# A negated copy and its accumulating DMA ahead of the high part, and a way-down product one slot sooner, in a float32 encoder trunk on one core

## The chip, the cores and the metric

The kernel runs on one core of one Trainium2 chip. The metric is the device time of one execution in microseconds (us); smaller is better. A time below is either the median of several runs or that of the one execution that the profiler recorded.

## The reference

Two layers on 512 tokens of width 1024, all in float32. Each layer is: a half-step SwiGLU feed-forward network (FFN), a mixer (an mLSTM in layer 0, a gated MLP in layer 1), a second half-step FFN, and a gated per-layer input (PLE). After each of them comes a layer norm of the scaled residual.

```python
def swiglu_ffn(x, w_gu, w_d):
    g, u = jnp.split(x @ w_gu, 2, axis=-1)
    return (jax.nn.silu(g) * u) @ w_d
...
x = layer_norm(DN_ALPHA * x + 0.5 * swiglu_ffn(x, ffn1_wgu[i], ffn1_wd[i]), ln_g[i, 0], ln_b[i, 0])
x = layer_norm(DN_ALPHA * x + mix, ln_g[i, 1], ln_b[i, 1])
x = layer_norm(DN_ALPHA * x + 0.5 * swiglu_ffn(x, ffn2_wgu[i], ffn2_wd[i]), ln_g[i, 2], ln_b[i, 2])
ple = jax.nn.sigmoid(x @ ple_wg[i] + ple_bg[i]) * (p[i] @ ple_wp[i])
x = layer_norm(DN_ALPHA * x + ple, ln_g[i, 3], ln_b[i, 3])
```

The hidden width of an FFN is 2816, that is 22 blocks of 128. There are four FFNs: the first and third come before a mixer and are called *plain* here, the second and fourth come before a PLE.

## The kernel before

**Two-part products.** A float32 product is made of three fp32r products (`mm3`, L386): high by high, high by low and low by high. Each weight tile is split for this: the high part `whi` is a rounding copy on ScalarE (ACT, L275), the low part `wlo` is the weight less its high part. The low part is made in one of two ways. Either VectorE (DVE) subtracts (L284, or L290 where it is put off), or "by DMA": ACT writes a negated copy of the weight into `wlo` (L281), and GpSimd (POOL) issues a DMA that adds the weight to it (L282); the tile's type rounds the copy, so what is left is the low part.

**The order of the weights.** The class `Weights` (L50) holds one list for the whole program, `W.order`. `fill` (L247) goes through it strictly in order: it takes the next entry if a split tile of its kind is free ("main": 4 tiles, "rows": 2, "rowsx": 1 and others) and if its load has been issued, and it stops at the first entry that can't be had. So whenever a product has given its tile back with `W.release`, the splits of later weights are queued on ACT, far ahead of their use, behind whatever ACT was given before. Loads go through SyncE's (SP's) queue; a load's place among three raw tiles comes free when the splits of what stood there are done (`load`, L184). While `W.apart` is set, which it is in the chunks named next, a low part that DVE makes is put off: `W.lows` (L303) does it at the next slot, in order. In this state `fill` also stops at a load that was issued in the last two slots (L257).

**The FFN.** The hidden blocks go in six chunks of 2, 4, 4, 4, 4, 4 blocks. From the third chunk on (index 2, `UP_FROM`), `up_products` (L1128) makes the way up of four blocks in 14 slots, s = 0 to 13. They are two pairs of blocks with seven products each, r = s mod 7, a Strassen-like scheme of seven products in place of eight. I call the up product of slot s U0 to U13. Woven between them are the seven products of the way down of the chunk before, by the same scheme; I call them G1 to G7. Before the change, G comes after the up product of every odd slot, so G7 comes after U13.

In a slot the program gives out, in this order: the up product on TensorE (PE); `group.add` (L973), which adds the G of an earlier slot to the residual `xt` on DVE (L763); for r = 6 the gating of the first half of the tokens (`gated(1)`, which needs nothing of U13: DVE L1104, then a split, ACT and DVE, L393 and L394); `pair.take(r)`, which takes the product out (for r = 6 this is `gated(0)`, the second half by the same steps); `W.lows`; `W.release`, which fills; the SiLU where r is 1 or 5 (L1099); and where a G belongs to the slot, `group.product`, `W.release(kind="rows")`, which fills again, and the next form.

**Which low parts are by DMA.** `up_forms` (L129) marks them by r: 1, 3, 4, 5, 6 in a chunk's first pair, 1, 3, 5, 6 in its second. Elsewhere (mLSTM and gated MLP) `release(low="dma")` does so.

**The end of the FFN.** In the last chunk the way down of its own four blocks is made by `down` (L789), right after slot 13. It goes over four blocks of tokens, t = 0 to 3, with four weights each, d0 to d3, two matmul triples for each. `hs` is what `gated` has split: d2 and d3 are multiplied by what slots 7 to 13 made. The weights d0 to d3 come from two loads (two weights each), and their kinds are main, rows, rowsx, rows in a plain FFN and rowsx, rows, main, main ahead of a PLE. In W.order they stand after the weight of G7, and ahead of a PLE a pair of transposes of p (`turn_p`, tile `ptp`) stands between. After d3 come the weights of the next stage: the input projection of the mLSTM or the gated MLP in a plain FFN, `ple_wp` ahead of a PLE.

## Time and profile before

| | |
|---|---|
| median of 3 runs | 2194.01 us (2192.73 to 2197.59) |
| the profiled execution | 2193.39 us |
| its span, first to last instruction | 2191.7 us |
| TensorE (PE) busy | 2170.3 us, 99% of the span |
| VectorE (DVE) busy | 1760.5 us, 80% |
| ScalarE (ACT) busy | 1208.1 us, 55% |
| GpSimd (POOL) busy | 226.3 us, 10% |
| granted TensorE clock | 0.999 |

A profile page gives the busy time of each engine, the chain of work that ended last, and groups of instructions by source line. A matmul row names its tiles: `ups` is an up product of the last four chunks, `gps` a way-down product of the scheme, `dps` a product of `down`, and `wlo`, `whi` the two parts of a weight. In a timeline row the numbers are the start within the span and the duration, both in us, and in brackets the idle time of the engine before it and what ended that. Rows of one kind that follow each other are merged, with their count behind the x; a q behind an engine's name means that the row is an issue of a DMA.

### The profile page before, as it was taken

Reading aid. Unit: us, or ns where it says so; the run is one execution under the profiler, and the core shown is the slowest. Engines: PE = TensorE matmul, PEld = TensorE weight load, DVE = VectorE, ACT = ScalarE, POOL = GpSimd, SP = SyncE. Lnnn points to the kernel's source line nnn. Section 1 sums busy time; section 2 is a strip of 40 time slices with the busy share of each in tenths; the row PEclk is TensorE's granted clock in tenths of the full one; section 3 lists DMA queues with packets and bytes.
Section 4 is the critical chain, followed back from the end, with each engine's and each line's share of the span. In section 5 each row is a group of like instructions: output and inputs, shape, how many; then the busy total and the mean of one; then the engine's idle time right before and its main releaser. Section 6 shows DMA issues by size and latency. Waiting matters only on the chain.

```text
span 2191.7 us, 32537 instructions
## 1 busy us (share of the span) xinstructions
PE 2170.3 (99%) x12821; PEld 1922.0 (88%) x12821; DVE 1760.5 (80%) x2532; ACT 1208.1 (55%) x1668; POOL 226.3 (10%) x279
## 2 busy tenths in 40 slices
PE   9999999999999999999999999999999999999998
PEld 8899997888888889999888899997888888999987
DVE  5898877786767789888887998877788679988887
ACT  4576656454546445667444566655345553666642
POOL 1011100011101101111000011110001100111100
PEclk9999999999999999999999999999999999999999
DMA  6587764366857426887531587754437743777651
GB/s 187 156 204 184 172 153 136 92 154 128 155 130 154 135 81 163 200 194 172 173 125 58 153 207 186 176 145 135 144 77 140 168 135 116 179 191 179 135 183 58
DMA packets 228097, 329.46 MB, mean 150 GB/s; under 512 B 9140, under 2 KB 163892, under 8 KB 227944
## 3 DMA queue, kind: packets, MB, share of 16 engines
q1 hardware_dynamic: 169104, 211.83, 29.8%
q0 software_dynamic: 52224, 100.86, 27.5%
q10 hardware_dynamic: 6616, 14.69, 1.9%
q8 instruction: 101, 1.65, 0.3%
q14 instruction: 52, 0.43, 0.1%
HBM read 224.58 MB, written 2.11 MB: 103 GB/s over the span
## 4 chain that ended last, share of the span: by engine, by line
PE 78%; DVE 11%; issue 4%; ACT 4%; DMA 3%; SPq 0%; POOL 0%; DVEq 0%; ACTq 0%; POOLq 0%
PE ups L390 7%; PE ups L388 7%; PE ups L389 7%; PE gps L388 6%; PE gps L389 6%; PE gps L390 6%; DMA wlo<-wbox 2%; PE dps L389 2%; PE dps L390 2%; PE dps L388 2%; DVE wlo L290 2%; PE fps L388 2%; PE fps L389 1%; PE fps L390 1%; ACT whi L275 1%
## 5 line engine op out<-in xcount | busy, mean ns | idle before, releaser
L275 ACT ACTIVATE whi<-wbox 128x1024 fp32r<-128x1024 f32 x224 | 235.7, 1054 | 242.2 <-DVE wbox L141 96.9
L390 PE MATMUL ups<-xh,wlo 128*128 128x256 f32 x1024 | 290.3, 284 | 3.2 <-DMA wlo<-wbox 3.2
L388 PE MATMUL ups<-xh,whi 128*128 128x256 f32 x1024 | 289.9, 283 | 0.0
L389 PE MATMUL ups<-xl,whi 128*128 128x256 f32 x1024 | 289.7, 283 | 0.0
L275 ACT ACTIVATE whi<-wraw 128x1024 fp32r<-128x1024 f32 (+1 forms) x212 | 217.3, 1046 | 96.7 <-DVE wraw L119 22.6
L388 PE MATMUL gps<-whi,fhi 128*128 128x512 f32 x644 | 253.0, 393 | 0.4
L389 PE MATMUL gps<-wlo,fhi 128*128 128x512 f32 x644 | 252.2, 392 | 0.0
L390 PE MATMUL gps<-whi,flo 128*128 128x512 f32 x644 | 251.4, 390 | 0.0
L282 POOL DMA_DIRECT2D wlo<-wbox x144 | 122.2, 848 | 1076.8 <-ACT wlo L281 705.0
L763 DVE TENSOR_TENSOR xt<-xt,gps 128x512 f32<-128x512 f32 x302 | 194.9, 680 | 26.7 <-PE gps L390 26.7
L284 DVE TENSOR_TENSOR wlo<-wraw,whi 128x1024 fp32r<-128x1024 f32 (+1 forms) x140 | 167.6, 1214 | 41.8 <-ACT whi L275 40.9
L390 PEld LDWEIGHTS ups<-xh,wlo 128*128 128x128 f32 x1024 | 196.2, 192 | 4.3 <-DMA wlo<-wbox 4.2
L388 PEld LDWEIGHTS ups<-xh,whi 128*128 128x128 f32 x1024 | 196.1, 192 | 3.8 <-ACT us L1085 1.6
L389 PEld LDWEIGHTS ups<-xl,whi 128*128 128x128 f32 x1024 | 196.1, 192 | 2.3
L275 ACT ACTIVATE whi<-wquarter 128x1024 fp32r<-128x1024 f32 (+1 forms) x140 | 135.3, 966 | 77.0 <-DVE wquarter L119 28.9
L281 ACT ACTIVATE wlo<-wbox 128x1024 fp32r<-128x1024 f32 x144 | 150.4, 1044 | 0.0
L390 PEld LDWEIGHTS gps<-whi,flo 128*128 128x128 f32 x644 | 120.9, 188 | 26.9
L388 PEld LDWEIGHTS gps<-whi,fhi 128*128 128x128 f32 x644 | 121.3, 188 | 23.9 <-issue 1.6
L389 PEld LDWEIGHTS gps<-wlo,fhi 128*128 128x128 f32 x644 | 121.3, 188 | 21.6
L944 DVE TENSOR_TENSOR flo<-h,fhi 128x512 fp32r<-128x512 f32 (+1 forms) x140 | 88.5, 635 | 57.6 <-ACT fhi L941 57.0
L290 DVE TENSOR_TENSOR wlo<-wquarter,whi 128x1024 fp32r<-128x1024 f32 x104 | 126.6, 1218 | 0.0
L388 PE MATMUL fps<-xh,whi 128*128 128x512 f32 x288 | 112.2, 390 | 0.0
(365 smaller groups left out, 5822.4 us busy)
## 6 DMA issues: line engine op xcount, KB each, us to landing
wlo<-wbox POOLq DMA_DIRECT2D x144, 512.0 KB, 5.8
wbox<-in_ffn_wgu_dram SPq DMA_DIRECT2D x128, 512.0 KB, 4.9
wquarter<-in_ffn_wd_dram SPq DMA_DIRECT2D x64, 512.0 KB, 5.8
wraw<-in_ml_w_in_dram SPq DMA_DIRECT2D x24, 1024.0 KB, 5.8
wlo<-wraw POOLq DMA_DIRECT2D x48, 512.0 KB, 6.4
wraw<-in_ffn_wgu_dram SPq DMA_DIRECT2D x15, 1024.0 KB, 6.0
wraw<-in_gm_w_in_dram SPq DMA_DIRECT2D x15, 1024.0 KB, 5.6
wraw<-in_ffn_wgu_dram SPq DMA_DIRECT2D x17, 512.0 KB, 4.8
```

Of the source, the lines that this page charges most:

```text
L275: self.nc.scalar.activation(hi[:, s], src[:, s], AF.Copy)
L281: self.nc.scalar.activation(lo[:, s], src[:, s], AF.Copy, scale=-1.0)
L282: self.nc.gpsimd.dma_start(lo[:, s], src[:, s], accum_op=OP.add)
L284: self.nc.vector.tensor_sub(lo[:, s], src[:, s], hi[:, s].bitcast(F32))
L290: self.nc.vector.tensor_sub(lo, src, hi.bitcast(F32))
L388: mm(ps, st[0], mv[0], start=start, stop=False, skip_group_check=more)
L389: mm(ps, st[0], mv[1], start=False, stop=False, skip_group_check=more)
L390: mm(ps, st[1], mv[0], start=False, stop=stop, skip_group_check=more)
L763: vec.tensor_add(dst, dst, ps)
L944: vec.tensor_sub(lo, src, hi.bitcast(F32))
```

## The change

Three edits. First, in `fill`, a low part by DMA has its negated copy and its DMA issued before the high part's copy; before, the high copy came first. Second, in the second pair of the last chunk, the low part of r = 5 (U12) is no longer by DMA; DVE subtracts it, at the next `W.lows`. Third, in the last chunk G7 comes after U12, not after U13, and its weight stands before that of U13 in W.order.

```diff
@@ -45,6 +45,7 @@
 UP_BY_DMA = (1, 3, 4, 5, 6)
 UP_BY_DMA_2 = (1, 3, 5, 6)
+UP_BY_DMA_LAST = (1, 3, 6)
@@ -272,15 +273,16 @@
             for i in range(parts):
                 s = slice(i * shape[1] // parts, (i + 1) * shape[1] // parts)
+                by_dma = make in self.by_dma or low == "dma" and make not in self.in_place
+                if by_dma:
+
+                    self.nc.scalar.activation(lo[:, s], src[:, s], AF.Copy, scale=-1.0)
+                    self.nc.gpsimd.dma_start(lo[:, s], src[:, s], accum_op=OP.add)
                 self.nc.scalar.activation(hi[:, s], src[:, s], AF.Copy)
                 if meanwhile and make in self.in_place:
                     meanwhile()
                     meanwhile = None
-                if make in self.by_dma or low == "dma" and make not in self.in_place:
-
-                    self.nc.scalar.activation(lo[:, s], src[:, s], AF.Copy, scale=-1.0)
-                    self.nc.gpsimd.dma_start(lo[:, s], src[:, s], accum_op=OP.add)
-                elif not self.apart:
+                if not by_dma and not self.apart:
                     self.nc.vector.tensor_sub(lo[:, s], src[:, s], hi[:, s].bitcast(F32))
@@ -471,6 +473,10 @@
+    def down_after(c, s):
+
+        return s == 12 if c == LAST and s > 11 else s % 2 == 1
@@ -499,10 +505,10 @@
-                                            by_dma=UP_BY_DMA if b == starts[c] else UP_BY_DMA_2)
+                                            by_dma=UP_BY_DMA if b == starts[c] else UP_BY_DMA_2 if c < LAST else UP_BY_DMA_LAST)
                 for s, product in enumerate(products):
                     W.order.append(product)
-                    if s % 2:
+                    if down_after(c, s):
                         W.order.append(down_w.popleft())
@@ -1147,7 +1153,7 @@
                     W.release()
                     pair.gate(r)
                     W.form_ahead(3)
-                    if s % 2:
+                    if down_after(c, s):
                         group.product()
                         W.release(kind="rows")
                         group.form(True)
```

## The prediction

> **What bounds the kernel now.** I read the page first, then what TensorE (PE) waits for, then the timelines of the four FFN ends, engine by engine.

> ```profile
> span 2191.7 us, 32537 instructions
> PE 2170.3 (99%) x12821; PEld 1922.0 (88%) x12821; DVE 1760.5 (80%) x2532; ACT 1208.1 (55%) x1668; POOL 226.3 (10%) x279
> PE dps L389 <- DVE wlo L290: 4.8, 4, 1.6
> PE ups L390 <- DMA wlo<-wbox: 3.9, 6, 1.0
> PE ups L390 <- DMA wlo<-wbox: 0.3, 1, 0.3
> PE ups L390 <- DMA wlo<-wbox: 0.5, 1, 0.5
> PE ups L390 <- DMA wlo<-wbox: 0.4, 1, 0.4
> ```

> PE is busy or pipelined nearly all the time, and none of its work goes away: the change can only take or add waits of PE. Two kinds bear on it (third and fourth line: total us, times, longest). `down` waits once in each FFN for a low part made by DVE, and six up products wait for an accumulating DMA. The last three lines are windows of the third chunk (first, second and fourth FFN); the other three of the six lie in the last chunks, at U12.

> A matmul's row is longer than its pitch, so each such idle time hides a little more delay. The rows:

> ```profile
> 1052.48 0.28 PE L388 MATMUL ups<-xh,whi 128*128 128x256 f32 x1
> 1055.36 0.28 PE L388 MATMUL ups<-t_whi,whi 128*128 128x256 f32 x1
> 1077.35 0.40 PE L388 MATMUL gps<-whi,fhi 128*128 128x512 f32 x1
> 1079.87 0.39 PE L390 MATMUL gps<-whi,flo 128*128 128x512 f32 x1
> 1080.10 0.39 PE L388 MATMUL dps<-whi,wquarter 128*128 128x512 f32 x1
> 1081.47 0.50 PE L388 MATMUL dps<-whi,wquarter 128*128 128x512 f32 x1
> 1082.86 0.50 PE L389 MATMUL dps<-wlo,wquarter 128*128 128x512 f32 x1 [0.89 <-DVE wlo L290]
> ```

> The first two span an up product: 24 matmuls in 2.88 us, 0.12 each against 0.28 shown, so an idle time stands for 0.16 more. The next two and the first `dps` row are G7 of the second FFN: 2.75 us, its last matmul starting 2.52 after its first. Each weight of `down` takes 1081.47 - 1080.10 = 1.37 for t = 0. The last row is d1, whose low part comes late: 1.39 after its high product, where 0.23 is the pitch, so 1.16 lost.

> **Edit 1, the copy and its DMA first.** ACT does the same two copies in the other order, so the DMA leaves one copy earlier and the high part is ready one copy later:

> ```profile
> 1061.05 1.05 ACT L281 ACTIVATE wlo<-wbox 128x1024 fp32r<-128x1024 f32 x1
> 1063.00 1.05 ACT L275 ACTIVATE whi<-wbox 128x1024 fp32r<-128x1024 f32 x1
> 1063.95 1.05 ACT L281 ACTIVATE wlo<-wbox 128x1024 fp32r<-128x1024 f32 x1
> 1053.77 0.84 POOL L282 DMA_DIRECT2D wlo<-wbox  x1 [12.13 <-ACT wlo L281]
> 1062.39 0.85 POOL L282 DMA_DIRECT2D wlo<-wbox  x1 [7.78 <-ACT wlo L281]
> 1065.29 0.84 POOL L282 DMA_DIRECT2D wlo<-wbox  x1 [2.04 <-ACT wlo L281]
> DMA to landing us min/median/max: 4.5/4.5/4.5
> DMA to landing us min/median/max: 9.3/9.3/9.3
> DMA to landing us min/median/max: 8.9/8.9/8.9
> ```

> Copies follow each other by 0.95 (1063.00, 1063.95), and POOL issues 0.29 after the copy's end. The three landings belong to the three issues, in order. The DMA thus leaves 0.95 earlier. A high part that is 0.95 later costs PE nothing: it is needed two matmuls before the low part, which lands 4.5 us or more after its issue. The third chunks' waits are 0.3 + 0.5 + 0.4 = 1.2 idle and, with 0.16 each, 1.7 in all, each shorter than 0.95. I credit all of it, **-1.7**; the other bound is 0, if those transfers were slow for want of room and not for their start.

> **Edit 2, U12's low part by DVE.** ACT loses a copy of 0.95 four times, DVE gains a subtraction of 1.14 (its pitch, rows below). It falls in slot 9, behind the low parts of slot 8; DVE idles for 2.10 us soon after (row below), which is its cover; without it the cost were 4 x 1.14 = 4.6.

> ```profile
> 1066.49 0.69 DVE L944 TENSOR_TENSOR flo<-h,fhi 128x512 fp32r<-128x512 f32 x1 [2.10 <-ACT fhi L941]
> 1062.13 10.06 SPq L239 DMA_DIRECT2D wraw<-in_ffn_wd_dram  x2
> ```

> U12's waits go: 3.9 - 1.2 = 2.7 idle, 3.2 with the pitch. And the second load of `down`'s weights, which stood waiting for the end of that DMA (second issue of SP's row, 10.06 - 0.37 after 1062.13, so 1071.8, where the DMA of 1062.39 landed), can go near 1064.4: two DVE subtractions (2 x 1.14) after the first load, which leaves at the end of U11's.

> **Edit 3, G7 after U12.** The "rows" tile that G7 gives back comes sooner. But `W.release(kind="rows")` does not fill one tile: it fills in order until a kind runs out. Before, this happened in slot 13 after both gatings had been given to ACT and DVE. After, it happens in slot 12, ahead of them. Since G7 no longer blocks the list, ACT gets, ahead of PE's last up product, in a PLE FFN d1, d2, d3 and the first `ple_wp` part (three "main" tiles are free, only U13 holds one), in a plain one d3 and the first two parts of the next projection. The limit on fresh loads does not stop them: that load was issued in slot 10, and in slot 12 only one from slot 11 or later is refused. Then come the splits of `gated(1)` and `gated(0)`, and DVE makes the low parts of `down`'s weights only after those (`W.lows` stands behind `take`). The profile of before shows both the cadence and what a late load does to ACT:

> ```profile
> 1077.13 0.63 ACT L393 ACTIVATE wquarter<-us 128x512 fp32r<-128x512 f32 x1 [1.11 <-DVE us L1104]
> 1080.36 4.85 ACT L275 ACTIVATE whi<-wraw 128x1024 fp32r<-128x1024 f32 x5 [0.61 <-PE gps L390]
> 1079.78 0.69 DVE L394 TENSOR_TENSOR wquarter<-us,wquarter 128x512 fp32r<-128x512 f32 x1 [0.70 <-ACT wquarter L393]
> 1081.59 5.76 DVE L290 TENSOR_TENSOR wlo<-wraw,whi 128x1024 fp32r<-128x1024 f32 x5
> 325.23 1.06 ACT L275 ACTIVATE whi<-wraw 128x1024 fp32r<-128x1024 f32 x1 [6.00 <-DMA wraw<-in_ffn_wd_dram]
> 326.19 0.61 ACT L1099 ACTIVATE us<-us 128x512 f32<-128x512 f32 x1
> 330.71 2.93 ACT L275 ACTIVATE whi<-wraw 128x1024 fp32r<-128x1024 f32 x3
> 333.92 0.50 PE L389 MATMUL dps<-wlo,wquarter 128*128 128x512 f32 x1 [1.60 <-DVE wlo L290]
> ```

> The SiLU at 326.19 stood behind a high copy that waited 6.00 for its load: so will the gating. In a PLE FFN the sum from the last start of G7 to d1's low product is: 0.49 to the first copy (1079.87 to 1080.36), four copies at 0.95 = 3.80, the two gatings from the first ACT split to the last DVE one 3.34 (1077.13 to 1079.78 + 0.69), the low part 1.14 ((5.76 - 1.22) / 4, one taking 1.22), 0.06 to PE (1082.80 to 1082.86): **8.83**. PE itself would be there after 0.23 + 2.88 + 1.37 + 0.23 = 4.71, so it waits 4.1.

> ```profile
> 1070.25 0.37 PE L388 MATMUL ups<-xh,whi 128*128 128x256 f32 x1
> 2092.36 0.37 PE L388 MATMUL ups<-xh,whi 128*128 128x256 f32 x1
> 2103.95 0.50 PE L389 MATMUL dps<-wlo,wquarter 128*128 128x512 f32 x1 [0.89 <-DVE wlo L290]
> 1074.24 0.37 SPq L239 DMA_DIRECT2D wraw<-in_ple_wp_dram  x1
> DMA to landing us min/median/max: 8.4/8.4/8.4
> 321.93 12.33 SPq L239 DMA_DIRECT2D wraw<-in_ml_w_in_dram  x3
> DMA to landing us min/median/max: 6.9/6.9/6.9
> ```

> U12 starts at 1070.25 in the second FFN and at 2092.36 in the fourth. The last start of G7 is then 2.88 + 2.52 later, plus 0.08 for the slower first matmul: 1075.73 and 2097.84. With 8.83, d1's low product comes at 1084.56 and 2106.67, against 1082.86 and 2103.95: **+1.7 and +2.7**, U12's old waits included.

> This holds if `ple_wp` has landed when ACT reaches it, at 1079.1 in the second FFN. Its load waits for U13's accumulate: before, issue 1065.29, landing 1074.2, load at 1074.24, landing 8.4 later (fifth line). After, U13's copy starts at 1063.0 (the list puts G7's weight ahead of it, U12's copy is gone), so the issue moves by only 0.96, and the freed second load now travels beside it. Estimate: accumulate landed at 1072 to 1073.5, `ple_wp` another 6 to 8 us later, 1078 to 1081. I add 0.4 to each: **+2.1 and +3.1**; bounds 0 and 3.6 (landing at 1082.66 as before).

> [...] The landings of 4.5 alone and 9.3 beside one load of twice its size fit a sharing no better than a queue.

> In a plain FFN only d3's low part is late (333.92 in the first). Its chain hangs on the load L of the next projection: two copies 1.90, gatings 3.34, low 1.14, ACT's and PE's starts 0.1: L + 6.5. Before, L was 321.93 + 6.9 = 328.8. After, it is issued at 320.3 to 322 and shares with the norm's two loads, which ACT now issues about then (L719, L720): L = 326 to 328.8, so 332.5 to 335.3 against 333.92. Were L early, PE itself would set the place: 333.92 less this wait (1.60 + 0.27) and U12's (1.0 + 0.16) is 330.9. I take **+0.3** for each of the two, near the middle of what L gives; bounds -3.0 and +1.4.

> **Sum.** -1.7 + 0.3 + 0.3 + 2.1 + 3.1 = **+4.1 us** on the profiled 2193.39 (span 2191.7 and 1.7 around it): 2197.5. That execution was 0.6 below the median of the three runs, so for a median 2194.0 + 4.1 = **2198.1**. A measurement of this kernel tells apart about 0.2%, 4.4 us; the forecast lies just inside.

> **Rivals.** *The waits simply go* (the changed kernel as its parts read): if the copies of slot 12 don't delay the gating, U12's 3.2, `down`'s 4.8 + 4 x 0.27 = 5.9 and the third chunk's 1.7 all vanish: 2194.0 - 10.8 = 2183.2. Against it stands the SiLU of 326.19: ACT doesn't overtake. 8%. *The next stage's loads are late*: U13's accumulate gets behind both loads and lands no earlier than before. Then ACT holds the gating until the old landing (1074.24 + 8.4 = 1082.6), and d1 comes 5.5 later (copy 0.95, 3.34, 1.14, 0.1): 1088.1, +5.3; as much past its +1.7 in the fourth, +6.3; with +1.4 twice and -1.7, +12.7: 2206.7. It decides from a `ple_wp` landing later than 1079.1. For it: the 9.3 and 8.9 us landings; against it: one accumulate less in the queues. 13%, and slower. *The ends come out even*: the fill in slot 12 costs what U12 and d1 gained, and only the third chunk's 1.7 is left: 2192.3. 7%.

> **Numbers.** The forecast has 72%, with a spread of about 3 us either way from its bounds: a little over half of it within 0.2% (38%), 33% slower, 1% faster. With the rivals: faster by over 0.2% 1 + 8 = 9%, within 38 + 7 = 45%, slower 33 + 13 = 46%; the forecast itself stands at the bound. The range leaves out the first rival and the far end of the second: 2192.0 to 2204.0; the forecast's own is 2194.5 to 2201.5.

> **What would show it.** Right: no wait of PE for `wlo<-wbox` of note; in the second and fourth FFN four high copies on ACT directly ahead of the two gating splits, and PE waiting some 4 us at d1's `dps` for DVE L290; in the plain ones a high copy that waits for the next projection's load, then d3 late by about 2. Wrong: gating splits on ACT at the end of U13 with the copies behind them, `dps` waits under 1 us; or, for edit 1, third-chunk waits that are still there.

## The result, and the profile after

The changed kernel takes 2216.15 us (median of 6 runs, 2206.98 to 2218.25), the kernel before, on the same chip, 2195.12 us (6 runs, 2192.73 to 2197.59). The ratio is 1.0089, 95% interval 1.0070 to 1.0108: slower by 21 us where 4 were forecast, and above the range given.

The changed kernel's profiled execution took 2213.05 us. First its page, then what TensorE waits for (total us, times, longest):

```profile
span 2211.3 us, 32474 instructions
PE 2175.1 (98%) x12821; PEld 1926.2 (87%) x12821; DVE 1765.7 (80%) x2536; ACT 1204.3 (54%) x1664; POOL 223.9 (10%) x275
```
```profile
PE dps L391 <- DVE wlo L292: 12.2, 4, 5.9
PE dps L390 <- ACT wquarter L395: 10.0, 2, 5.0
PE ups L392 <- DMA wlo<-wbox: 0.9, 1, 0.9
```

PE runs the same 12821 matmuls. The waits for an accumulating DMA fell from 3.9 to 0.9 us, and those of `down` rose from 4.8 to 22.2: four for a low part, as before, and two new ones for the gated product itself. (Line numbers have moved: `mm3` is now L390 to L392, the copy of the high part L281, the negated copy and its DMA L279 and L280, the subtraction that is put off L292, the gating split L395 and L396; lines further down have moved by 6.)

The timeline of the changed kernel at the end of the second FFN, SP and POOL, then ACT, DVE and PE:

```profile
1068.17 0.84 POOL L280 DMA_DIRECT2D wlo<-wbox  x1 [10.65 <-ACT wlo L279]
1065.96 2.59 SPq L240 DMA_DIRECT2D wraw<-in_ffn_wd_dram  x2
1078.20 0.37 SPq L240 DMA_DIRECT2D wraw<-in_ple_wp_dram  x1
...
1080.03 2.95 ACT L281 ACTIVATE whi<-wraw 128x1024 fp32r<-128x1024 f32 x3 [1.45 <-PE gps L392]
1084.81 1.06 ACT L281 ACTIVATE whi<-wraw 128x1024 fp32r<-128x1024 f32 x1 [1.83 <-DMA wraw<-in_ple_wp_dram]
1085.78 0.61 ACT L395 ACTIVATE wquarter<-us 128x512 fp32r<-128x512 f32 x1
1087.74 0.63 ACT L395 ACTIVATE wquarter<-us 128x512 fp32r<-128x512 f32 x1 [1.35 <-DVE us L1110]
...
1089.01 3.49 DVE L292 TENSOR_TENSOR wlo<-wraw,whi 128x1024 fp32r<-128x1024 f32 x3
...
1074.08 0.37 PE L390 MATMUL ups<-xh,whi 128*128 128x256 f32 x1
1090.29 0.79 PE L391 MATMUL dps<-wlo,wquarter 128*128 128x512 f32 x1 [5.87 <-DVE wlo L292]
```

Read it upwards from the last row: PE waits 5.87 for d1's low part, DVE makes that after the gating, ACT splits the gating after four high copies (three and one), and the fourth stood 1.83 for `ple_wp`, whose load SP could issue only at 1078.20. The DMA answers of the changed kernel give what SP stood behind (KB, us from issue to landing; U13's accumulate, the second load of `down`'s weights, `ple_wp`, and `ml_w_in` in the first FFN):

```profile
wlo<-wbox POOLq DMA_DIRECT2D x1, 512.0 KB, 10.0
wraw<-in_ffn_wd_dram SPq DMA_DIRECT2D x1, 1024.0 KB, 10.1
wraw<-in_ple_wp_dram SPq DMA_DIRECT2D x1, 1024.0 KB, 6.6
wraw<-in_ml_w_in_dram SPq DMA_DIRECT2D x1, 1024.0 KB, 9.0
```

The accumulate left at 1068.17, within 0.02 of the second load, and landed 10.0 later, at 1078.1; `ple_wp` left then and landed 6.6 later, at 1084.8. In the first FFN it is the same, with `ml_w_in`, issued at 321.98 and landed at 331.01:

```profile
331.04 2.00 ACT L281 ACTIVATE whi<-wraw 128x1024 fp32r<-128x1024 f32 x2 [6.39 <-DMA wraw<-in_ml_w_in_dram]
332.95 0.61 ACT L395 ACTIVATE wquarter<-us 128x512 fp32r<-128x512 f32 x1
...
317.18 0.28 PE L390 MATMUL ups<-xh,whi 128*128 128x256 f32 x1
333.61 0.80 PE L390 MATMUL dps<-whi,wquarter 128*128 128x512 f32 x1 [5.03 <-ACT wquarter L395]
334.21 0.63 PE L391 MATMUL dps<-wlo,wquarter 128*128 128x512 f32 x1
337.46 0.50 PE L391 MATMUL dps<-wlo,wquarter 128*128 128x512 f32 x1 [0.57 <-DVE wlo L292]
```

The 19.6 us between the two spans, by place. An end is measured from U12's first matmul to the low product that comes late (d3's in a plain FFN, d1's ahead of a PLE); what lies between the ends is the rest.

| | before | after | difference | forecast |
|---|---|---|---|---|
| first FFN's end (plain) | 16.00 | 20.28 | +4.28 | +0.3 |
| second (PLE) | 12.61 | 16.21 | +3.60 | +2.1 |
| third (plain) | 15.32 | 20.16 | +4.84 | +0.3 |
| fourth (PLE) | 11.59 | 15.60 | +4.01 | +3.1 |
| behind the second's and fourth's late product | | | +2.33, +1.58 | |
| between the other ends | | | -0.74, +0.29, -0.59 | -1.7 in all |

The two entries behind the late products are something that no part of the prediction has. The page by windows of the changed kernel there (length, busy times, then the granted clock third from the end):

```profile
1084.00:1087.00 3.00, 0.42 (x2) 0.00 (x0) 0.58 (x1) 1.58 (x2) 0.00 (x0) 1.00 0.01 3
1087.00:1088.00 1.00, 0.00 (x0) 0.00 (x0) 0.71 (x2) 0.26 (x1) 0.00 (x0) 0.80 0.00 0
1088.00:1091.00 3.00, 0.71 (x2) 0.62 (x3) 2.60 (x3) 1.32 (x2) 0.00 (x0) 0.50 0.00 0
1091.00:1094.00 3.00, 3.00 (x9) 2.32 (x8) 3.00 (x4) 0.00 (x0) 0.00 (x0) 0.50 0.84 259
1094.00:1095.00 1.00, 1.00 (x5) 0.81 (x4) 0.77 (x1) 0.00 (x0) 0.00 (x0) 0.79 1.07 410
1095.00:1096.00 1.00, 1.00 (x6) 0.80 (x6) 0.29 (x1) 0.00 (x0) 0.00 (x0) 1.00 1.02 385
```

The clock falls to half during the wait, at 1087.60 (0.80 is 0.60 at 1 and 0.40 at 0.5), and comes back at 1094.42: 6.8 us. PE works in 4 of these, at a pitch of 0.43 where before it is 0.23 (0.43 is 1091.31 less 1090.88, the next matmuls' starts): 1.9 lost. In the fourth FFN it is 1.6. In the plain ends the half clock costs nothing, since d3 waits behind it in any case (0.57 at 337.46).

### The profile page after: what moved, and what is told of

It is laid out like the page before. It is cut to its first block, busy times and chain, and to the rows that moved or that the text cites. A ratio compares the mean times of both kernels' runs of the same rounds, so it can differ in the third digit from the quotient of the medians.

```text
span 2211.3 us, 32474 instructions
## 1 busy us (share of the span) xinstructions
PE 2175.1 (98%) x12821; PEld 1926.2 (87%) x12821; DVE 1765.7 (80%) x2536; ACT 1204.3 (54%) x1664; POOL 223.9 (10%) x275
## 4 chain that ended last, share of the span: by engine, by line
PE 78%; DVE 9%; ACT 5%; DMA 4%; issue 3%; POOL 0%; DVEq 0%; ACTq 0%; SPq 0%; POOLq 0%
PE ups L392 7%; PE ups L390 7%; PE ups L391 7%; PE gps L390 6%; PE gps L391 6%; PE gps L392 6%; DMA wlo<-wbox 3%; ACT whi L281 3%; PE dps L391 2%; PE dps L392 2%; PE fps L390 2%; PE fps L392 2%; PE fps L391 2%; PE dps L390 2%; DVE wlo L292 1%
## 5 line engine op out<-in xcount | busy, mean ns | idle before, releaser
L281 ACT ACTIVATE whi<-wbox 128x1024 fp32r<-128x1024 f32 x224 | 235.0, 1049 | 169.0 <-DVE wbox L142 96.5
L390 PE MATMUL ups<-xh,whi 128*128 128x256 f32 x1024 | 290.0, 283 | 0.5
L392 PE MATMUL ups<-xh,wlo 128*128 128x256 f32 x1024 | 289.7, 283 | 0.0
L281 ACT ACTIVATE whi<-wraw 128x1024 fp32r<-128x1024 f32 (+1 forms) x212 | 217.2, 1045 | 96.0 <-DVE wraw L120 22.6
L390 PE MATMUL gps<-whi,fhi 128*128 128x512 f32 x644 | 253.0, 393 | 0.5 <-DVE xt L767 0.2
L392 PE MATMUL gps<-whi,flo 128*128 128x512 f32 x644 | 251.4, 390 | 0.0
L280 POOL DMA_DIRECT2D wlo<-wbox x140 | 119.0, 850 | 1075.3 <-ACT wlo L279 879.2
L390 PEld LDWEIGHTS ups<-xh,whi 128*128 128x128 f32 x1024 | 196.2, 192 | 4.5 <-ACT us L1091 2.2
L392 PEld LDWEIGHTS ups<-xh,wlo 128*128 128x128 f32 x1024 | 196.3, 192 | 0.0
L279 ACT ACTIVATE wlo<-wbox 128x1024 fp32r<-128x1024 f32 x140 | 147.5, 1053 | 75.6 <-PE ups L392 39.8
L281 ACT ACTIVATE whi<-wquarter 128x1024 fp32r<-128x1024 f32 (+1 forms) x140 | 135.3, 966 | 74.9 <-DVE wquarter L120 28.9
L392 PEld LDWEIGHTS gps<-whi,flo 128*128 128x128 f32 x644 | 120.9, 188 | 26.8
L390 PEld LDWEIGHTS gps<-whi,fhi 128*128 128x128 f32 x644 | 121.3, 188 | 24.0 <-issue 1.6
L292 DVE TENSOR_TENSOR wlo<-wquarter,whi 128x1024 fp32r<-128x1024 f32 x104 | 126.7, 1218 | 0.0
L390 PE MATMUL fps<-xh,whi 128*128 128x512 f32 x288 | 112.2, 390 | 0.0
```

The lines of the kernel that those rows point to most:

```text
L279: self.nc.scalar.activation(lo[:, s], src[:, s], AF.Copy, scale=-1.0)
L280: self.nc.gpsimd.dma_start(lo[:, s], src[:, s], accum_op=OP.add)
L281: self.nc.scalar.activation(hi[:, s], src[:, s], AF.Copy)
L292: self.nc.vector.tensor_sub(lo, src, hi.bitcast(F32))
L390: mm(ps, st[0], mv[0], start=start, stop=False, skip_group_check=more)
L392: mm(ps, st[1], mv[0], start=False, stop=stop, skip_group_check=more)
```

## The experiments

Theory A: edit 3 makes the loss, because slot 12 now fills weights ahead of the gating. Theory B: edit 1 does, since its DMAs leave sooner and get in the way of loads. Theory C: edit 2 does, since it frees the second load of `down`'s weights to run beside U13's accumulate. Later letters stand in the expectations. Each run's median is beside the median of before on the same chip (2194.46 for e1 to e4, 2194.39 for e5 to e8, 2194.61 for e9 to e11, 2194.36 for e12).

**e1, edit 1 alone**, `UP_BY_DMA_2` in the last chunk and `s % 2 == 1` in `down_after`.

> Edit 1 alone (the negated copy and its DMA first; the low part of U12 still by DMA, G7 still after U13). Theory A, that edit 3 makes the loss by filling next-stage weights ahead of the gating: edit 1 gives 0 to -2 us against before, time 2193 to 2195, granted clock as before. Rival B, that the DMAs which leave sooner get in the way of the loads: slower by 5 us or more.

Measured: 2188.05, ratio 0.9967 (0.9954 to 0.9979), -6.4 us. What e1's PE waits for:

```profile
PE dps L390 <- DVE wlo L291: 3.5, 4, 1.1
PE ups L391 <- DMA wlo<-wbox: 1.1, 2, 0.8
```

B falls, and A's 0 to -2 is passed: edit 1 is a gain, and a larger one than was thought. It took away all three waits at U12, which the forecast gave to edit 2, and 1.3 of `down`'s. In the third chunks it took away hardly anything: two waits of 0.84 and 0.22 in place of 0.28, 0.51 and 0.38.

**e2, edit 2 alone**: `UP_BY_DMA_LAST` kept, the two copies in the old order and the old `down_after`.

> Edit 2 alone (the low part of U12 by DVE). Theory A: faster by 2 to 6 us; the waits at U12 are gone, the second load of the down weights leaves some 7 us sooner, and a wait of up to 1 us comes up at U13, whose accumulate now travels beside that load. Rival C, that this freed load is what makes the loss (it crowds out U13's accumulate and all that hangs on it): not faster, with waits of 2 us or more at U13.

Measured: 2187.94, 0.9971 (0.9960 to 0.9982), -6.5 us. U12's waits go here too, but U13 gets some:

```profile
323.50 0.39 PE L391 MATMUL ups<-t_f,wlo 128*128 128x256 f32 x1 [1.59 <-DMA wlo<-wbox]
```

In the first FFN the accumulate of U13 left at 313.51, beside the freed load of 313.53, and landed 9.9 later. That is C's mechanism, at 1.6 us, and C's "not faster" falls. (The profiled execution, 2190.91, is the slowest of the seven.)

**e3, edit 3 alone**:

```diff
+        return s == 12 if c == LAST and s > 11 else s % 2 == 1
...
-                    if s % 2:
+                    if down_after(c, s):
                         W.order.append(down_w.popleft())
...
-                    if s % 2:
+                    if down_after(c, s):
                         group.product()
```

> Edit 3 alone (G7 after U12). Theory A: slower by 15 to 22 us, with waits of 4 to 7 us in each of the four FFN ends and a granted clock of 0.5 after them, since ACT takes next-stage weights ahead of the gating and the second load comes as late as before. Rival C: within 4 us of before, since no load is freed.

Measured: 2213.38, 1.0083 (1.0068 to 1.0098), +18.9 us, `dps` waits of 17.4 us in four places, the longest 7.2. Edit 3 makes the loss, and C falls. A's 4 to 7 us and half clock are seen ahead of a PLE alone (6.89 and 7.16); the plain ends wait 1.70 and 1.68 for the low part, at full clock.

**e8, edits 1 and 3 without edit 2**: `UP_BY_DMA_2` in the last chunk again.

> Edits 1 and 3 without edit 2: U12's low part by DMA again. The second down load then waits for that DMA. Theory A: as slow as the changed kernel or slower (2214 to 2224), with ACT held by loads in all four ends. Rival C, that the freed second load delays U13's accumulate: faster than the changed kernel by 5 us or more, and U13's accumulate lands sooner after its issue.

Measured: 2206.57, 1.0058 (1.0043 to 1.0073), +12.2 us, so 9 us less than all three edits. A's number is missed. Both signs of C come true: U13's accumulate lands 6.7, 8.6, 6.7 and 6.1 after its issue, against 9.8, 10.0, 9.5 and 9.2 in the changed kernel. But the freed load is only a part of the loss, since 12 us are left without it. The timeline of e8, the late products of the first and second FFN:

```profile
333.46 0.50 PE L391 MATMUL dps<-wlo,wquarter 128*128 128x512 f32 x1 [1.72 <-DVE wlo L292]
1087.29 0.80 PE L391 MATMUL dps<-wlo,wquarter 128*128 128x512 f32 x1 [6.93 <-DVE wlo L292]
```

From U12 (317.59 and 1070.01) these are 15.87 and 17.28, against 20.28 and 16.21 after. So, with edit 3 in place, the freed load costs about 4 us in each plain end (the third: 16.17 against 20.16), and nothing ahead of a PLE, where the wait is as long without it (the fourth: 15.48 against 15.60).

**e4, slot 12 doesn't fill**: the changed kernel, the "rows" tile given back at the end of slot 13.

```diff
                         group.product()
-                        W.release(kind="rows")
+                        if c < LAST or s != 12:
+                            W.release(kind="rows")
                         group.form(True)
+                    if c == LAST and s == 13:
+                        W.release(kind="rows")
```

> The changed kernel, but the rows tile that G7 gives back in slot 12 is filled only at the end of slot 13, where it was filled before. Theory A: the long waits of the FFN ends and the half clock are gone, faster than before by 3 to 8 us (2187 to 2192). Rival C (loads and accumulates in each other's way): still slower than before by 5 us or more, as every load and DMA leaves as in the changed kernel.

Measured: 2190.54, 0.9981 (0.9972 to 0.9991), -3.9 us: 25 less than the changed kernel, with G7 still after U12. It is the fill of slot 12 that costs, not the place of G7 on PE. C, which had it still slower, falls. The long waits are gone; a half clock of 3.4 us is left in the second FFN.

**e5, slot 12 fills only `down`'s own weights** (three ahead of a PLE, one in a plain FFN).

```diff
-                        W.release(kind="rows")
+                        if c == LAST and s == 12:
+                            W.free["rows"] += 1
+                            W.fill(1 if prepare is None else 3)
+                        else:
+                            W.release(kind="rows")
```

> The changed kernel with the fill of slot 12 limited to the weights of down itself (three ahead of a PLE, one in a plain FFN), so that no next-stage weight stands on ACT ahead of the gating. Theory A: in the plain FFNs no wait over 1 us is left; ahead of a PLE d1 still waits some 3 us, since its low part stays behind the gating; the clock stays at 1.0; 2189 to 2194. Rival C: 2210 or more, as the loads are as in the changed kernel.

Measured: 2192.98, 0.9996 (0.9986 to 1.0005), no difference from before that these runs can tell. No next-stage weight stands ahead of the gating, and the large waits are gone; the three copies of `down`'s own weights do, and d1 still waits 2.98 in both PLE ends, with 3.4 us of half clock after it, where A had the clock at 1.0.

**e7, e5 with the low parts made in time**: in slot 13 of the last chunk `W.lows(1)` before `gated(1)`, `W.lows()` between the two gatings.

> As the limited fill, and in slot 13 of the last chunk DVE makes the first pending low part before the gating of the first half and the others between the two gatings. Theory A: no wait of PE over 1 us is left in the FFN ends; faster than before by 6 to 10 us (2185 to 2189). Rival C: slower than before.

Measured: 2188.19, 0.9973 (0.9964 to 0.9983), -6.2 us. `down` doesn't wait at all any more. **e10** is the same without edit 2:

> Edits 1 and 3, with the fill of slot 12 limited to `down`'s own weights and the low parts of these made ahead of and between the two gatings; U12's low part by DMA as before. Theory N (with the waits of `down` gone, the next to be late is DVE's residual and norm behind `down`, and it takes back what `down` gives): no `dps` wait, waits of 0.8 to 1.5 at the transposes after `down`, 2186 to 2189. Rival P (those waits come from edit 2, which gives DVE four more subtractions just there): the transposes don't wait, and it is 2182 to 2185.

Measured: 2188.75, 0.9974 (0.9964 to 0.9984), -5.9 us. The timeline of e10 behind `down` of the second FFN:

```profile
1089.52 1.29 PE L637 MATMUL xps<-ident,xt 128*128 128x128 f32 x8 [1.31 <-DVE xt L752]
```

N holds, P falls: the transposes of the next stage now wait for DVE's norm, in both kernels (1.32 and 1.30 in e7, 1.31 and 1.30 in e10). DVE was full behind `down` already in the kernel before (third busy time, 6.00 of 6.00):

```profile
1080.00:1086.00 6.00, 5.12 (x23) 3.81 (x22) 6.00 (x7) 4.85 (x5) 0.00 (x0) 1.00 0.44 153
```

So PE's wait for d1, once removed, comes back some 12 us later (d1's low product is at 1077.35 in e10).

**e6, the clock kept up**: the changed kernel with 40 transposes of the identity ahead of `down` in each FFN, for which nothing waits.

> The changed kernel with 40 transposes of the identity on PE (results unused) between slot 13 and down in each FFN, about 4 us of work that fills most of the wait. If the half clock after a long wait costs what its windows say (about 7 us in all): 2207 to 2211. If the clock is only a sign and costs nothing: 2216 as the changed kernel. If the waits were short and only the clock made them: the added work shows, 2220 or more.

Measured: 2206.73, 1.0060 (1.0045 to 1.0075), +12.3 us, some 9 less than the changed kernel though PE does more. The granted clock is 1.00 through all four ends. Behind d1's low product the matmuls of `down` up to the next transposes take 10.60 and 10.56 in the two PLE ends, as before (10.54 twice), where the changed kernel takes 12.47 and 12.10: that is the half clock, 3.4 in all. The two profiled executions are 6.7 apart. The rest is not the clock: the four ends are 3.6 shorter, since the loads landed at other times too (`gm_w_in` 7.3 after its issue instead of 9.2).

**e11, U13's low part by DVE too**: `UP_BY_DMA_LAST = (1, 3)`, so that no accumulate stands ahead of the next stage's load.

> The changed kernel with U13's low part by DVE too, so that the next stage's first load stands behind no accumulating DMA; the fill of slot 12 runs as far ahead as in the changed kernel. Theory L (the loss is the landing of that load: d1 comes 5.5 after it, d3 6.5 after it): the load is issued some 2 us after the second load of `down`'s weights and has landed when ACT reaches it; d1 waits 3 to 4.5 as the forecast's chain had it, d3 under 1: -0.9, -3.0 twice, +1.7, +2.7 make -2.5, 2192, and up to 2196 if the half clock comes with these waits. Rival F (the copies of slot 12 themselves are the loss, whenever the load lands): 2206 or more, and waits over 5 us.

Measured: 2201.15, 1.0029 (1.0017 to 1.0040), +6.5 us, above L's 2192 to 2196 and below F's 2206. The DMA answer of e11 for `ple_wp` of the second FFN, and two rows of its timeline:

```profile
wraw<-in_ple_wp_dram SPq DMA_DIRECT2D x1, 1024.0 KB, 5.1
```
```profile
1080.41 0.80 PE L391 MATMUL dps<-wlo,wquarter 128*128 128x512 f32 x1 [2.99 <-DVE wlo L292]
1106.11 0.50 PE L391 MATMUL pwp<-wlo,whi 128*128 128x512 f32 x1 [1.79 <-DVE wlo L286]
```

The load left at 1065.29 and had landed before ACT came to it. But the fill does not run as far ahead as the expectation says. ACT in the second FFN:

```profile
1073.03 2.96 ACT L281 ACTIVATE whi<-wraw 128x1024 fp32r<-128x1024 f32 x3 [1.45 <-PE gps L392]
1075.88 0.62 ACT L395 ACTIVATE wquarter<-us 128x512 fp32r<-128x512 f32 x1
1077.86 0.63 ACT L395 ACTIVATE wquarter<-us 128x512 fp32r<-128x512 f32 x1 [1.36 <-DVE us L1110]
```

The three copies are `down`'s own; `ple_wp` comes after the gating, and so do the projection's copies in the plain ends. (A likely reason, read from the code and not tested: U13's put-off subtraction gives its raw tile back later, so the next load is still too fresh for slot 12.) So e11 is e5 in this respect, and can't tell L from F: what a next-stage copy ahead of the gating costs when its load has landed in time is not shown by any run. From U12 (317.25, 1067.07, 1474.63, 2093.45) d3's, d1's, d3's and d1's low products came after 13.46, 13.34, 13.47 and 13.33 (e5: 13.37, 13.33, 13.80, 13.34): -2.5, +0.7, -1.9 and +1.7 against before, -1.9 in all, where L had -1.6 (-3.0 twice, +1.7, +2.7). The forecast's chain is seen in it: G7's last matmul at 1072.54, d1 7.87 later, and 8.83 less one copy of 0.95 is 7.88 (three copies stood ahead of the gating here, not four). What spoils the total is new: the PLE's first low products wait for DVE, 1.79 twice, and with the clock, which halves again at both places, they cost about 4 in each PLE (its first 24 matmuls take 9.33 and 9.36 for 5.21 and 5.22 before). Without these 8 it were 2193, in L's range, but e11 can't bear L out. The lead of the early plain ends is kept (PE is 3.2 ahead of before at d3 of the first FFN and at U12 of the second). The weight of the landing is seen in the changed kernel itself: ACT, with the gating behind it, stands idle for the four loads for 6.39, 1.83, 6.80 and 1.21, 16.2 in all, where the four ends are 16.7 longer.

**e12, the changed kernel once more.**

> The changed kernel once more, unaltered; its runs lie 11 us apart (2206.98 to 2218.25), those of the kernel before 5. Theory L: in each PLE end d1's low product starts 5.5 after the landing of the next stage's first load, in each plain end d3's 6.5 after it, within 0.1, whatever the landing is this time, and a profiled time other than 2213.05 differs by what the four landings differ by (counted from U12's start) and by the half clock. Rival V: the landings are the same within 0.5, and a difference in time lies elsewhere.

Measured: 2214.34, 1.0092 (1.0075 to 1.0108). The four loads landed at 329.26, 1085.11, 1492.29 and 2114.28, and the late products came at 335.71, 1090.61, 1498.74 and 2119.78: 6.45, 5.50, 6.45 and 5.50 later, as in the first profile (6.45, 5.50, 6.44, 5.50). V falls: counted from U12 the landings of the plain FFNs came 1.8 and 2.4 earlier than in the first profile. But the time hardly fell with them (2211.82 profiled): the four ends are 4.0 shorter in all, and the half clock, which now lay where it cost 2.0 in the first FFN too and 1.0 more in the fourth, took 2.8 of that back.

**e9, edits 1 and 2 without edit 3**: the old `down_after`.

> Edits 1 and 2 without edit 3. Theory L (edit 3 is the loss; each of the other two takes U12's wait away, and they can take it away only once): no wait at U12, waits of about 0.8 to 1.1 at d1 or d3 as with either alone, small ones at U13: 2185 to 2189, so no better by more than 2 us than either alone. Rival S (their gains add up): 2194.4 - 6.4 - 6.5 = 2181.5, with the waits of `down` gone as well.

Measured: 2185.59 (2185.46 to 2186.13), 0.9960 (0.9947 to 0.9972): -9.0 us, 2.4 beyond either alone, and the best of all. S's 2181.5 isn't reached, and L's bound of 2 us beyond either alone is passed, though its 2185 to 2189 holds: U12 and U13 don't wait, the plain ends don't either, and what is left in the ends are two waits at d1. Against e9 the changed kernel is 30 us slower: with the other two edits in place, edit 3 costs more than the 18.9 that it costs alone. The timeline of e9 in the second FFN:

```profile
1078.04 0.50 PE L391 MATMUL dps<-wlo,wquarter 128*128 128x512 f32 x1 [0.89 <-DVE wlo L292]
```

## Why the prediction was wrong, point by point

**Edit 3's mechanism was right.** Four high copies ahead of the gating splits in a PLE FFN with d1 late by DVE L292, a high copy that waits for the next projection's load in a plain one with d3 late: all of it is in the trace. In a plain end, though, most of PE's wait stands one step earlier in the same chain, at d2 for the gated product itself (5.03 and 4.92, against 0.57 and 0.52 at d3), which the prediction had not named. Its two formulas hold to 0.06: d1 5.50 after `ple_wp`'s landing (5.5 in the prediction), d3 6.45 after the projection's (6.5). e4 shows that this fill is the loss.

**The step that failed is the landing in a plain FFN**, "L = 326 to 328.8", and the +0.3 taken from it, with +1.4 as its upper bound. L was 331.01. The prediction speaks of the freed second load beside U13's accumulate only in the PLE ends; in a plain end it leaves with it too, the accumulate takes 9.8 from its issue, and SP issues the projection's load behind it at the old time (321.98 against 321.93), the late edge of the 320.3 to 322 that was forecast, though PE is 0.74 earlier there. The term that was mis-sized is that load's own flight: it took 9.03, where a landing by 328.8 leaves 6.8 for it (6.88 before). The prediction named the norm's two loads beside it and gave them no price. That is +4.3 and +4.8 instead of +0.3 twice: 8.5 of the 15.5 that were missed; the PLE ends are 2.4 of it, what lies behind their late products 3.9, and the places between the other ends 0.7. e8 confirms it: without edit 2 the first flight is 6.75, and these ends are about 4 us shorter.

**The PLE ends** were mis-sized by less: +3.6 and +4.0 for +2.1 and +3.1, so that the late `ple_wp` added 1.9 and 1.3 to the chain's +1.7 and +2.7, where the prediction added 0.4 with bounds of 0 and 3.6. The estimate "accumulate landed at 1072 to 1073.5" was too early. Moved back by the 3.83 by which PE was late, the accumulate landed at 1074.3 (before: 1074.2) and `ple_wp` at 1081.0. So the rival "the next stage's loads are late" is what happened, by its own mechanism (the accumulate lands no earlier than before) and past its point of decision (1079.1), if less late than it had; it had been given 13%, and the range left its 2206.7 out. Where a 1 MB load left with the 512 KB accumulate, the accumulate took 9.2 to 10.0 us in the changed kernel, against 4.5 without one (issued at 1056.65, landed at 1061.20).

**Edit 1's -1.7** was credited to the third chunks, and they gave about 0.6 (idle 1.2 to 0.9, and with 0.16 for each wait 1.7 to 1.1). In the second FFN the DMA that PE had waited for landed in time, but the next one, which left sooner too, landed at 897.95 as late as before (894.12, with PE 3.78 behind by then), and PE now waits 0.94 for that: here the bound of 0 was the right one. It left at 888.34, 0.93 sooner by the same count, and the DMA engines' mean busy share was 1.05 from then to its landing; that want of room held it up is not shown. The edit is worth 6.4 by itself, for the most part by U12 and `down`, but on top of edit 2 only about 2.4. The prediction had U12's wait going with edit 2, so its sum is not hurt by this.

**The half clock was missing**: 1.9 and 1.6 us behind the PLE waits of the profiled run. In four other runs the clock was low for longer: the mean granted clock is 0.992 in those that take 2215.83 to 2218.25, 0.995 in the profiled one, 0.996 in the one of 2206.98. What that cost there no trace shows. How the 21 us of the median divide between landing and clock is therefore known only for the profiled run, 19.6 slower: 16.7 at the ends, 3.5 by the clock, -0.6 elsewhere.

**Why the loss was not the same everywhere**: the landing of the four loads depends on what leaves ahead of them, as e8 shows (the first projection's load took 6.75 there and 9.03 in the changed kernel). It also goes with the norm's two loads, which ACT issues within 0.03 us of the landing of the second load of `down`'s weights (322.09 in the changed kernel, 319.68 in e12). In the first FFN the projection's load took 8.4 to 9.1 where the first of these left within 0.5 us behind it (changed kernel, e2, e5), 6.8 to 6.9 where it left 2.5 or more behind (before, e1, e3, e8, e10), and 7.3 to 8.1 where it left 0.5 to 1.7 ahead (e4, e6, e7, e12). No run changes this alone, so it is not shown as the cause, and e9's 7.2 and e11's 5.5, both with 1.2 behind, fit no simple rule. Why the second load itself landed after 10.0 us in one run of the changed kernel and after 7.5 in another (e12) stays open.

## What to carry to other kernels

Freeing a buffer earlier is not free where one in-order filler acts on it: ask what else the filler will now hand to a busy engine, and whether any of it can stand there waiting for a load. Give back the buffer later, or limit the fill to what is due (e4, e5), before trusting a sooner product; here leaving the product in its place was best (e9). And when a chain hangs on one transfer, bound its landing with everything that the change lets travel beside it, in each place where the chain occurs, and take the far bound if the near one needs room on the queues.

## What the runs showed of the hardware

An accumulating DMA of 512 KB landed 4.5 us after its issue where no load left beside it (before, 1053.77), and 9.2 to 10.0 after it in the four ends of the changed kernel's profile, where a 1 MB load left within 0.02 us of it. That load took 9.5 to 10.2 there (7.5 in the first FFN of e12), where 5.1 was seen for one of its size (e11).
